# The RWKV recurrence of a two-layer decoder: a chunk's output turned by 64x64 identity products next to other 64x64 products, and y's last products moved beside the state's update

## The chip, the cores and the metric

The kernel runs on one NeuronCore of one Trainium2 chip. The metric is the device time of one execution in microseconds (us). Before the change it was 3168.34 us, the median of 3 runs that lay between 3163.14 and 3170.98. TensorE (PE) has a granted clock with two levels, 1.2 and 2.4 GHz, which the profile gives as 0.50 and 1.00.

## The reference, cut to what matters

Two layers on 2048 tokens of 1024 channels: sliding-window attention, then RWKV-7 time mixing, each followed by a gated embedding; a norm at the end. All is in float32. The change lies in the second layer, in the recurrence over tokens and the norm of its output per head:

```python
def step(S, inp):
    r_t, d_t, k_t, v_t, kk_t, a_t = inp
    sa = jnp.einsum('bhvk,bhk->bhv', S, -kk_t)
    S = S * d_t[:, :, None, :] + sa[..., None] * (kk_t * a_t)[:, :, None, :] + v_t[..., None] * k_t[:, :, None, :]
    y = jnp.einsum('bhvk,bhk->bhv', S, r_t)
    return S, y
...
y = ((y - mean) * lax.rsqrt(var + GN_EPS)).reshape(B, T, C) * gn_g + gn_b
y = (y + bonus.reshape(B, T, C)).astype(h.dtype)
return (y * jax.nn.silu(z)) @ w_out
```

## The kernel before, in words

The program has four phases: the projections of the attention layer, the attention, the projections of the RWKV layer, and `rwkv`, which is the phase of the change and runs from about 2000 us to the end.

In `rwkv` the 2048 tokens are 32 chunks of 64 tokens. The 16 heads are 8 pairs; the even head of a pair lives on partitions 0 to 63 and the odd one on 64 to 127 (`half`). What a chunk needs apart from the state is made ahead: `front` (masked products `aps`, transposes `tp`) for each chunk, and `tri` (inverses of triangular matrices, mostly small VectorE operations on `P` and `tmp`, and products `wq`) for four chunks at a time. The state then goes from chunk to chunk in `chain`, in five sets of 16 small products:

- `r1p` (L1307), what the chunk's tokens see of the state; ScalarE copies it to `r1`;
- the first part of `y` (L1313), from the state, 64x64 products, the even head's in one quarter of TensorE's array and the odd head's in the opposite one. I call it y's first products;
- `up` (L1317), the inverse times `r1`, also 64x64; VectorE and ScalarE copy it into `uv`;
- `sp` (L1324), the state's update, products of 128 rows and 64 columns; VectorE makes the next state from it (L1326, L1329) and GpSimd a copy (L1330);
- the last part of `y` (L1333), again 128 rows and 64 columns, added to the first in the one PSUM tile that `y` has. I call it y's last products.

Then `output` norms y: ScalarE squares (L1346), VectorE sums (L1348, L1349), GpSimd raises (L1350), VectorE scales y into `yc` (L1352). y's first products of the next chunk write the same PSUM tile, so they come after L1352 of this one. `yc` has tokens on partitions and has to be turned into [channel, token]: eight `transpose` instructions for the even heads (L1357) and eight products with an identity for the odd heads (L1358), taken in turn, into a PSUM tile `ytp`. `ytp` is one of three buffers of a pool that `aps`, `tp` and `wq` use too. VectorE multiplies it by a factor per channel (L1359), GpSimd adds and multiplies (L1361, L1362), and it goes to memory as `gated`.

Beside all that runs the generator `dense`: products of 128x128 weights with 512 tokens (`ps`, L567 to L569, three for each step because a float32 is split into two parts), which make z, the embeddings' projections, the output projection and the gate. One step of `dense` is a tick. `chain` calls `ticks(n)` between its sets of products, with n from `STEPS = (2, 2, 4, 3, 7)`, and at each tick every live generator (`front`, `tri`, `output`, `dense`) goes on to its next `yield`. So the written order of instructions comes from these counts; a scheduler in the framework then moves instructions within each engine by its own estimate of when their operands are ready. The order that results is the order of each engine's queue. VectorE, ScalarE and GpSimd run theirs in that order.

In `output` the ten yields ahead of the turning stand for ten ticks (four for the last chunk).

Of the kernel before, what the change touches and what calls it, by code (L numbers as in the profile page):

```python
# [16 lines left out]
T = 2048          # tokens  # L17
C = 1024          # channels
KT = C // 128     # 128-channel tiles
G = 512           # tokens of a group  # L20
# [27 lines left out]
def chan(ap, n):  # L48
    """A vector over channels as [128, n], channel = n_index * 128 + partition."""
    return ap.rearrange("(n p) -> p n", p=128)  # L50


class Dense:
    """A stream of matrix products with G tokens each, as a generator of steps (one k tile of one column of
    128): jobs (kind, n), whose operands of the tokens are fetched and split while the job before runs, and
    whose weights come in units of 8 steps."""

    def __init__(self, tr, es, name, jobs, side, raw=4, tmp=4, own=10, ps=2, lead=4):
        self.tr, self.nc, self.name, self.jobs = tr, tr.nc, name, jobs
        self.kinds = {}  # L60
        self.hp = tr.pool(es, name + "dh", 16, side=side)
        self.lp = tr.pool(es, name + "dl", 1, side=side)
        self.bufs = {"raw": raw, "t": tmp, "h": own, "m": ps}
        self.lead, self.cols_done, self.direct = lead, {}, {}
        # a job whose operands' last columns come from a tile on chip, [128, k, columns], once it is known
        self.late, self.rest = None, None
# [58 lines left out]
    def run(self):  # L125
# [5 lines left out]
        owner = []     # of each pair of operand tiles the last step that reads it  # L131
        for j, (kind, n) in enumerate(self.jobs):
            kt = self.kinds[kind].get("kt", KT)
            b = begin[kind, n] = 8 * len(units)
            units += [(kind, n, c) for c in range(self.kinds[kind].get("units", kt))]
            for k in range(kt):
                free = owner[len(owner) - KT] if len(owner) >= KT else -99
                if "after" in self.kinds[kind]:
                    # column k of that job, which has 8 units
                    fill = max(free + 1, begin[self.kinds[kind]["after"], n] + 8 * k + 8)  # L140
                else:
                    fill = max(free, b + k - 9) + 3
                    pre = 3 if "pre" in self.kinds[kind] else 0
                    if pre:
                        at(fill - pre, "pre", j, k)
                    at(fill - pre - self.lead, "fetch", j, k)
                assert fill <= b + k
                at(fill, "fill", j, k)
                if (kind, n) == self.late:
                    at(max(fill, b), "late", j, k)  # L150
                owner.append(8 * len(units) - kt + k)
# [6 lines left out]
        job = -1  # L158
# [48 lines left out]
    def add_ple(self, kind, i):  # L207
        """p @ w_proj / 2 of layer i."""
# [29 lines left out]
    def add_out(self, kind, w, src, res, ready, scale=None):  # L238
        """src @ w + res, which stay on chip for the job that follows; src is in memory or, as a function of the
        group and the k tile, on chip."""  # L240
# [10 lines left out]
    def add_rest(self, kind, src, m):  # L251
        """The last group's operands of a kind of jobs are in memory but for the last m columns."""
# [5 lines left out]
    def add_z(self, kind, w, src, dst):  # L258
        """Twice silu(lerp(src, src before, mu[3]) @ w)."""
# [12 lines left out]
        def pre(n, k, t):  # L272
            xs = self.tmp("xs")
            # GpSimd has other work while the phase starts
# [15 lines left out]
    def gated(self, th, ps, hl, ple, last=False):  # L290
        """h + sigmoid(ps) * 2 ple, where h = hi + lo."""
        nc = self.nc
        if last:
            # what does not need ps comes first
# [12 lines left out]
    def add_gate0(self, kind):  # L307
        """h2 = h1 + gated embedding of layer 0; hn1 = its norm."""
# [39 lines left out]
    def add_lora(self, kind):  # L348
        """Parts (float32r and the rest) of tanh(xw @ w1) and xa @ a1, from the products of hn1 and of hn1 a
        token earlier with weights that hold the lerps' factors."""  # L350
# [30 lines left out]
    def add_gate1(self, kind):  # L381
        """The result: the norm of h3 + gated embedding of layer 1."""
# [47 lines left out]
class Trunk:  # L430
# [40 lines left out]
    def consts(self):  # L471
        """Vectors of channels of the RWKV layer."""
# [21 lines left out]
    def lora_weights(self, pool, tag):  # L494
        """[w1 | a1] for hn1 a token earlier and for hn1, with the factors of the lerps."""
# [13 lines left out]
    def split(self, hi, lo, src, lo_engine="dve", scale=None):  # L509
        """hi (rounded to float32r) + lo = src exactly, or a power of two times it."""  # L510
# [9 lines left out]
    def rsqrt_rows(self, ss, s1, s2, op0, op1, pool, tag):  # L520
        """(ss op0 s1 op1 s2) ** -0.5 for a [128, G] PSUM tile whose rows are equal within each
        32 partitions: its 32 x 32 blocks are transposed so that only G / 32 columns are raised."""
# [12 lines left out]
    def operands(self, H, L, groups, pool):  # L535
        """Tiles (float32r and the rest) of the k tiles of groups of tokens."""
# [4 lines left out]
    # A phase is a generator: its first steps, which open the pools on the side of memory that the phase  # L541
    # before has left and start its first loads, run beside the end of that phase.
# [4 lines left out]
    # Work that goes on beside the matmuls is written as generators; each step of a matrix product  # L547
    # (one k tile) is a tick, in which every live one goes on to its next yield.
    def start(self, gen):
        """Runs gen to its first yield, and keeps it live."""  # L550
# [20 lines left out]
    def load_w(self, w, c0, lo_pool=None, lo_engine="dve"):  # L571
        """128 columns of a [C, n] weight as (hi, lo), [128, KT, 128] each."""
# [7 lines left out]
    def attn_proj(self):  # L580
# [8 lines left out]
        with ExitStack() as left, ExitStack() as right, ExitStack() as norms:  # L589
# [22 lines left out]
            def stats(n, wait=0):  # L612
                """1 / rms of a group's tokens, in a row that all partitions have."""
# [30 lines left out]
            def normed(n):  # L644
                """The group's operands: x transposed, normed and split."""
# [93 lines left out]
            for n in range(NG):  # L739
# [11 lines left out]
                # the first group's k tiles have just come about: all three products take each  # L751
# [27 lines left out]
    # ---- attention over blocks of 128 queries; beside it the embeddings' projections, the output  # L779
    # projection, the gated embedding of layer 0 and the norm of layer 1 ----  # L780
# [131 lines left out]
    def rwkv_proj(self):  # L912
# [6 lines left out]
        with ExitStack() as left, ExitStack() as right:  # L919
# [49 lines left out]
            def head_sums(sh, so):  # L969
                """Sums over each head's 64 channels, on all of its partitions (PSUM)."""  # L970
# [5 lines left out]
            def low_rank(j, nm, ct, n):  # L976
                """tanh(half of w0 + tanh(xw @ w1) @ w2) or of its like of a, in steps; n = 0 comes with the weights."""
# [35 lines left out]
            def evac_k(ps, ct, n):  # L1013
# [40 lines left out]
                # the products that the chunks' inverses need  # L1054
# [7 lines left out]
                # the diagonal 32 x 32 blocks of both halves of a chunk go into the same columns  # L1062
# [55 lines left out]
            for i, (c, evac) in enumerate(parts):  # L1118
                for pr in range(0, KT, 2):
                    if i or pr:  # L1120
                        ws = [self.load_w(w_in, c * C + ct * 128) for ct in (pr, pr + 1)]
                    for n in range(NG):
# [9 lines left out]
                        # the next part's operands: its first tiles are done with the last of this one, or,  # L1132
                        # where this one keeps the other engines busy, mostly with its own first
# [7 lines left out]
    # Of a pair of heads the even one lives on partitions 0-63 and the odd one on 64-127, so the  # L1141
    # operands stacked on 128 partitions are in the opposite order for the odd head.
    def rwkv(self):
# [9 lines left out]
        with ExitStack() as es:  # L1153
# [5 lines left out]
            # z is twice what it stands for  # L1159
# [23 lines left out]
            AM, X1, XA, BN, TT, UV, AG, BZ = {}, {}, {}, {}, {}, {}, {}, {}  # L1183

            def load_front(c):
# [5 lines left out]
                if c % 2 == 0:  # L1191
                    # [channel, pair, a or r, chunk, token] of two chunks
# [6 lines left out]
            def front(c):  # L1199
                """What chunk c needs apart from the state: masked products between its tokens, and the  # L1200
                transposes of x1."""
# [11 lines left out]
                # the products of the inverse are known: their place takes the operand of the state  # L1213
# [17 lines left out]
            def tri(g):  # L1231
                """Transposed inverses of I - A for the chunks of group g: first those of the 32 x 32
                diagonal blocks, one per partition (head, half of the chunk, pair, chunk)."""
# [65 lines left out]
            STEPS = (2, 2, 4, 3, 7)  # L1299

            def chain(c):
# [10 lines left out]
                for p, eo in pairs:  # L1312
                    mm(y[half[eo], p], lhsT=xa[half[eo], p, 1], rhs=uv[half[eo], eo, p], start=p == 0, stop=False)  # L1313
                self.ticks(STEPS[1])
# [16 lines left out]
                self.ticks(STEPS[3])  # L1331
# [3 lines left out]
                self.ticks(STEPS[4])  # L1335

            def load_bz(c):
                BZ[c] = tuple(r2.tile([128, NP, LC], F32, name=nm) for nm in ("bvt", "szt"))
                for t, src in zip(BZ[c], (bv, sz)):
                    nc.sync.dma_start(out=t, in_=src[:, c * LC:c * LC + LC].rearrange("(p q) t -> q p t", q=128))  # L1340

            def output(c, y):
# [10 lines left out]
                for _ in range(10 if c + 1 < NCH else 4):  # L1353
                    yield
                tp = p_f.tile([128, NP, LC], F32, name="ytp", tag="f")
                for p in range(NP):
                    nc.tensor.transpose(tp[half[0], p], yc[half[0], p], self.ident[half[0], half[0]])  # L1357
                    nc.tensor.matmul(tp[half[1], p], lhsT=yc[half[1], p], rhs=self.ident[half[1], half[1]], start=True, stop=True)  # L1358
# [63 lines left out]
```

## Time and profile before

| | |
|---|---|
| median of 3 runs | 3168.34 us |
| span of the profiled execution | 3165.9 us |
| PE matmul busy | 2989.6 us (94%) |
| VectorE busy | 2099.7 us (66%) |
| ScalarE busy | 1439.7 us (45%) |
| GpSimd busy | 1023.0 us (32%) |
| DMA, mean rate | 168 GB/s |
| stretch of the recurrence | about 2000 to 3040 us |
| dense products alone after it | 3040 to 3165.9 us |

The profiled execution's span, from its first to its last instruction, is 2.4 us under the median of the runs. Busy PE time is not PE at its peak, because products overlap; how fast a set of products goes is read from the difference between starts in the timeline. A float32 product is two PE instructions (two passes), so 16 products of a set stand as 32 instructions; a transpose is one. Line numbers are those of the kernel before.

### The profile page before, as it was taken

The numbers are of one execution on the slowest core, as the hardware profiler recorded it, in microseconds if no ns is written. First come the engines' busy times: TensorE is split into PE (matmuls) and PEld (weight loads), VectorE is DVE, ScalarE is ACT, GpSimd is POOL, SyncE is SP. The second block draws the span as 40 slices with busy tenths as digits, with TensorE's granted clock in tenths as the row PEclk, the third lists the DMA queues.
The fourth block names the chain that finished last, engine by engine and source line by source line (L and its number), as shares of the span: only waits on it lengthen the run. The fifth ranks groups of instructions, "written<-read, shape, count | busy, mean of one in ns | idle before, by whom it ended". The sixth has DMA issues, their size and how long they took to land. (4 is left out here: it accounts for less than half of the span.)

```text
span 3165.9 us, 55911 instructions
## 1 busy us (share of the span) xinstructions
PE 2989.6 (94%) x21160; PEld 2346.0 (74%) x21160; DVE 2099.7 (66%) x3665; ACT 1439.7 (45%) x2976; POOL 1023.0 (32%) x886
## 2 busy tenths in 40 slices
PE   7999997999999998898998899999999999999997
PEld 5888886777777776686776687777777777777776
DVE  6533434766888766747778867688777587684455
ACT  5311114864675544526677633333333443443433
POOL 2233500002211333305556501124634444453421
PEclk9999998999999989999998999998999999989999
DMA  7665838875674555636556778855566566566463
GB/s 217 191 134 119 170 124 222 234 203 168 160 200 114 163 174 163 190 117 196 178 198 203 219 201 211 232 142 140 145 161 144 131 158 169 132 157 161 108 190 93
DMA packets 704030, 532.84 MB, mean 168 GB/s; under 512 B 255504, under 2 KB 558736, under 8 KB 703760
## 3 DMA queue, kind: packets, MB, share of 16 engines
q1 hardware_dynamic: 696080, 518.76, 59.0%
q0 software_dynamic: 7680, 10.50, 3.0%
q8 instruction: 167, 2.74, 0.4%
q14 instruction: 103, 0.84, 0.1%
HBM read 350.09 MB, written 168.56 MB: 164 GB/s over the span
## 5 line engine op out<-in xcount | busy, mean ns | idle before, releaser
L567 PE MATMUL ps<-dhi,dwh 128*128 128x512 f32 x1472 | 614.9, 420 | 19.5 <-ACT dwh L516 14.6
L569 PE MATMUL ps<-dhi,dwl 128*128 128x512 f32 x1472 | 598.8, 407 | 12.1 <-DVE dwl L518 11.5
L568 PE MATMUL ps<-dlo,dwh 128*128 128x512 f32 x1472 | 599.0, 408 | 4.1 <-DVE dlo L518 2.5
L567 PE MATMUL ps<-xH,wh 128*128 128x512 f32 x1408 | 555.1, 401 | 20.4 <-DVE kb L1049 7.6
L568 PE MATMUL ps<-xL,wh 128*128 128x512 f32 x1408 | 559.8, 398 | 1.8 <-DVE xL L518 1.4
L569 PE MATMUL ps<-xH,wl 128*128 128x512 f32 x1408 | 560.4, 398 | 0.8 <-DVE wl L518 0.8
L567 PEld LDWEIGHTS ps<-dhi,dwh 128*128 128x128 f32 x1472 | 285.5, 194 | 90.9 <-ACT dwh L516 16.0
L569 PEld LDWEIGHTS ps<-dhi,dwl 128*128 128x128 f32 x1472 | 285.2, 194 | 80.5 <-DVE dwl L518 14.9
L568 PEld LDWEIGHTS ps<-dlo,dwh 128*128 128x128 f32 x1472 | 286.3, 194 | 63.5 <-POOL dlo L518 4.6
L567 PEld LDWEIGHTS ps<-xH,wh 128*128 128x128 f32 x1408 | 268.4, 192 | 83.1 <-DVE kb L1049 11.5
L568 PEld LDWEIGHTS ps<-xL,wh 128*128 128x128 f32 x1408 | 270.1, 192 | 61.6 <-DVE xL L518 2.4
L569 PEld LDWEIGHTS ps<-xH,wl 128*128 128x128 f32 x1408 | 269.4, 191 | 59.0 <-DVE wl L518 1.7
L518 DVE TENSOR_TENSOR dwl<-wraw,dwh 128x1024 fp32r<-128x1024 f32 x152 | 194.4, 1279 | 120.6 <-ACT dwh L516 113.8
L516 ACT ACTIVATE dwh<-wraw 128x1024 fp32r<-128x1024 f32 x152 | 160.5, 1056 | 202.4 <-PE ps L568 138.5
L677 POOL DMA_DIRECT2D t<-t x160 | 126.0, 1255 | 201.2 <-issue 78.8
L851 ACT ACTIVATE S<-S,nm 128x256 f32<-128x256 f32 (+1 forms) x256 | 125.6, 494 | 68.8 <-DVE nm L848 62.9
L518 POOL TENSOR_TENSOR xL<-xs,xH 128x512 fp32r<-128x512 f32 x72 | 111.2, 1554 | 69.3 <-ACT xH L516 68.9
L516 ACT ACTIVATE wh<-wr 128x1024 fp32r<-128x1024 f32 x44 | 46.6, 1060 | 185.8 <-DMA wr<-in_attn_w_in 141.4
L842 DVE CUSTOM_DVE_ANT_0 S<-sc,mask,sink 128x256 f32<-128x256 f32 (+1 forms) x256 | 109.0, 468 | 20.8 <-PE sc L838 20.7
L1247 DVE TENSOR_TENSOR tmp<-P 128x30 f32<-128x30 f32 (+14 forms) x240 | 111.7, 465 | 9.3 <-POOL P L1238 3.4
L953 DVE SCALAR_TENSOR_TENSOR xs<-hp,mu,xs 128x512 f32<-128x512 f32 x96 | 94.1, 991 | 31.1 <-ACT xs L952 30.6
L1249 DVE TENSOR_TENSOR P<-P,tmp 128x30 f32<-128x30 f32 (+14 forms) x240 | 108.8, 454 | 6.4
(260 smaller groups left out, 5517.8 us busy)
## 6 DMA issues: line engine op xcount, KB each, us to landing
wraw<-in_ple_w_gate SPq DMA_DIRECT2D x64, 512.0 KB, 4.0
hp<-hn SPq DMA_DIRECT2D x72, 256.5 KB, 4.0
sz<-th SPq DMA_DIRECT2D x64, 256.0 KB, 4.5
ple<-pt SPq DMA_DIRECT2D x64, 256.0 KB, 6.0
wraw<-in_attn_w_out SPq DMA_DIRECT2D x32, 512.0 KB, 4.0
aux<-ple SPq DMA_DIRECT2D x64, 256.0 KB, 3.8
yd<-kx SPq DMA_DIRECT2D x32, 512.0 KB, 4.4
wraw<-in_rwkv_w_in SPq DMA_DIRECT2D x32, 512.0 KB, 5.3
```

Of the source, the lines that this page charges most:

```text
L516: nc.scalar.activation(hi, src, AF.Copy)
L518: e.tensor_tensor(out=lo, in0=src, in1=f32(hi), op=ALU.subtract)
L567: mm(ps, lhsT=wh, rhs=ah, start=first, stop=False)
L568: mm(ps, lhsT=wh, rhs=al, start=False, stop=False)
L569: mm(ps, lhsT=wl, rhs=ah, start=False, stop=last)
L677: nc.gpsimd.dma_start(out=t1[32 * d:32 * d + 32, :], in_=t2[32 * a:32 * a + 32, :], accum_op=ALU.add)
L842: nc.vector.tensor_tensor_reduce(out=S[:, i, c0:], in0=sc[:, eo, c0:], in1=mask[:, c0:], scale=1.0, scalar=sink[:, 4 * g + 2 * j + eo:4 * ...
L851: nc.scalar.activation(S[:, i, c0:], S[:, i, c0:], AF.Exp, bias=nm[:, i:i + 1], accum_out=den[:, i:i + 1])
L953: nc.vector.scalar_tensor_tensor(out=src, in0=t[:, :G], scalar=mus[:, c, k:k + 1], in1=src, op0=ALU.mult, op1=ALU.add)
L1247: nc.vector.tensor_tensor(out=t, in0=P[:, 0:r, r:r + 1].broadcast_to([128, r, n]), in1=P[:, r:r + 1, r + 1:].broadcast_to([128, r, n]), op ...
L1249: nc.vector.tensor_tensor(out=P[:, 0:r, r + 1:], in0=P[:, 0:r, r + 1:], in1=t, op=ALU.add)
```

## The change

- `output` no longer issues the turning itself, but for the last chunk. It puts `yc` into a table and yields until the turned tile is there.
- A new function `turn` turns a chunk with 16 identity products, for the even and odd heads alike; no `transpose` is left. `chain` of the next chunk calls it right after y's first products.
- `chain` issues y's last products right after the state's update, without the three ticks between them; the three are added to the seven at the end.

```diff
-            STEPS = (2, 2, 4, 3, 7)
+            STEPS = (2, 2, 4, 10)
...
                 for p, eo in pairs:
                     mm(y[half[eo], p], lhsT=xa[half[eo], p, 1], rhs=uv[half[eo], eo, p], start=p == 0, stop=False)
+                if c:
+                    turn(c - 1, YC.pop(c - 1))
                 self.ticks(STEPS[1])
...
                     nc.gpsimd.tensor_tensor(out=S, in0=t, in1=d, op=ALU.mult)
-                self.ticks(STEPS[3])
                 for p, eo in pairs:
                     mm(y[half[eo], p], lhsT=am[:, p, eo, LC:], rhs=uv[:, eo, p], start=False, stop=p == NP - 1)
                 self.start(output(c, y))
-                self.ticks(STEPS[4])
+                self.ticks(STEPS[3])
...
+            def turn(c, yc):
+                tp = YT[c] = p_f.tile([128, NP, LC], F32, name="ytp", tag="f")
+                for p in range(NP):
+                    for h in half:
+                        nc.tensor.matmul(tp[h, p], lhsT=yc[h, p], rhs=self.ident[h, h], start=True, stop=True)
...
-                for _ in range(10 if c + 1 < NCH else 4):
-                    yield
-                tp = p_f.tile([128, NP, LC], F32, name="ytp", tag="f")
-                for p in range(NP):
-                    nc.tensor.transpose(tp[half[0], p], yc[half[0], p], self.ident[half[0], half[0]])
-                    nc.tensor.matmul(tp[half[1], p], lhsT=yc[half[1], p], rhs=self.ident[half[1], half[1]], start=True, stop=True)
+                if c + 1 < NCH:
+                    YC[c] = yc
+                    while c not in YT:
+                        yield
+                else:
+                    for _ in range(4):
+                        yield
+                    turn(c, yc)
+                tp = YT.pop(c)
```

The rest of the diff is comments.

Two places of PE's queue show what moves. In its rows x16 counts 16 equal products in a row (each is two instructions in the trace).

The first is in the chain of chunk 12, which turns the output of chunk 11; `tp` is the front's transposes, `y<-uv,xa` are y's first products. Before:

```order
L1226 MATMUL tp<-ident,x_22758 128x128 x4
L1313 MATMUL y<-uv,xa 64x64 x16
L567 MATMUL ps<-dhi,dwh 128x512
L568 MATMUL ps<-dlo,dwh 128x512
L569 MATMUL ps<-dhi,dwl 128x512
L1357 MATMUL ytp<-ident,yc 64x64
L1358 MATMUL ytp<-ident,yc 64x64
```

and seven more pairs of L1357 and L1358, four transposes `tp` and one dense step follow ahead of `up`. Now:

```order
L1226 MATMUL tp<-ident,x_22758 128x128 x4
L1313 MATMUL y<-uv,xa 64x64 x16
L1348 MATMUL ytp<-ident,yc 64x64 x16
L567 MATMUL ps<-dhi,dwh 128x512
L568 MATMUL ps<-dlo,dwh 128x512
L569 MATMUL ps<-dhi,dwl 128x512
```

The dense step that stood between y's first products and the turning now comes after both, so the 32 products of 64x64 stand in one piece. Of the 31 turnings that `chain` calls, 28 stand right behind y's first products like this; three early ones stand a few rows later.

The second is around the state's update of chunk 18, where `wq` are `tri`'s 32x32 products. Before:

```order
L1268 MATMUL wq<-at,ag 32x32 x9
L1278 MATMUL wq<-tt,wt 32x32 x16
L1324 MATMUL sp<-uv,bn 64x64 x16
L1268 MATMUL wq<-at,ag 32x32 x7
L1333 MATMUL y<-uv,am 64x64 x16
L568 MATMUL ps<-dlo,dwh 128x512
```

and now:

```order
L1268 MATMUL wq<-at,ag 32x32 x14
L1278 MATMUL wq<-tt,wt 32x32 x16
L1268 MATMUL wq<-at,ag 32x32 x2
L1326 MATMUL sp<-uv,bn 64x64 x16
L1334 MATMUL y<-uv,am 64x64 x16
L567 MATMUL ps<-dhi,dwh 128x512
```

The update and y's last products stand in one piece now. In about one chunk of four they stood apart before; in the others the scheduler had put 15 of the 16 y products behind the update already. Counted along PE's queue from the recurrence's first `aps` to the end, the shape of the products (128x128 with any number of columns, 128x64, 64x64, 64x128, 32x32) changes 611 times before and 547 times now.

## Rows read from the trace of the kernel before

**Rows 1.** The page: its first line, and PE's line of the busy times.

```profile
span 3165.9 us, 55911 instructions
PE 2989.6 (94%) x21160; PEld 2346.0 (74%) x21160; DVE 2099.7 (66%) x3665; ACT 1439.7 (45%) x2976; POOL 1023.0 (32%) x886
```

**Rows 2.** Windows: stretch, us; busy us (instructions) of five engines; granted clock; DMA share; GB/s.

```profile
2000.00:3040.00 1040.00, 1005.08 (x11133) 775.24 (x11134) 735.94 (x1131) 399.91 (x810) 437.92 (x360) 0.93 0.60 150
3040.00:3165.90 125.90, 106.16 (x461) 83.94 (x459) 68.21 (x89) 42.15 (x122) 22.59 (x16) 0.93 0.50 147
2111.80:2327.30 215.50, 207.81 (x2439) 162.19 (x2438) 180.59 (x281) 78.04 (x135) 110.49 (x92) 0.89 0.57 142
2327.30:3018.60 691.30, 675.74 (x7711) 519.35 (x7710) 460.20 (x695) 271.38 (x582) 294.45 (x240) 0.94 0.59 146
```

**Rows 3.** PE's waits, 2000 to 3040 us: total us, times, longest us.

```profile
PE ps L569 <- DVE dwl L518: 6.8, 5, 2.4
...
PE y L1313 <- DVE yc L1352: 2.2, 1, 2.2
PE aps L1208 <- ACT am L1211: 1.8, 1, 1.8
```

**Rows 4.** PE's timeline in chunk 12: start us, us to the group's last end, what.

```profile
2436.24 1.15 PE L1313 MATMUL y<-uv,xa 64*64 64x64 f32 x32
2437.32 0.50 PE L567 MATMUL ps<-dhi,dwh 128*128 128x512 f32 x1
2437.66 0.40 PE L568 MATMUL ps<-dlo,dwh 128*128 128x512 f32 x1
2437.89 0.39 PE L569 MATMUL ps<-dhi,dwl 128*128 128x512 f32 x1
2438.21 0.24 PE L1357 MATMUL ytp<-ident,yc 64*64 64x64 f32 x1
2438.39 0.33 PE L1358 MATMUL ytp<-ident,yc 64*64 64x64 f32 x2
2438.64 0.24 PE L1357 MATMUL ytp<-ident,yc 64*64 64x64 f32 x1
...
2441.63 0.66 PE L1226 MATMUL tp<-ident,x 128*128 128x128 f32 x4
...
2443.41 1.97 PE L1317 MATMUL up<-r,tt 64*64 64x64 f32 x32
2445.32 0.65 PE L567 MATMUL ps<-dhi,dwh 128*128 128x512 f32 x1
```

**Rows 5.** The instructions on `ytp`: duration ns min/median/max, first and last start.

```profile
L1358 PE MATMUL ytp<-ident,yc x512: 218/267/365, 2113.1 to 3039.0; 64*64 64x64 f32 x171
L1357 PE MATMUL ytp<-ident,yc x256: 241/242/313, 2113.0 to 3038.8; 64*64 64x64 f32 x128
```

**Rows 6.** Windows of about 3.4 us: chunk 12's turning and the two after it.

```profile
2438.20:2441.60 3.40, 3.40 (x25) 2.34 (x24) 3.19 (x7) 0.00 (x0) 1.49 (x2) 1.00 0.22 64
2442.30:2445.60 3.30, 3.30 (x36) 2.43 (x36) 3.03 (x11) 0.59 (x1) 0.78 (x1) 0.50 0.49 114
2445.70:2449.10 3.40, 3.40 (x16) 2.71 (x16) 3.40 (x3) 0.75 (x1) 1.75 (x2) 1.00 0.62 131
```

**Rows 7.** Windows right behind the first and the last turning that a fall follows.

```profile
2170.00:2173.40 3.40, 3.40 (x38) 2.81 (x35) 1.76 (x4) 0.59 (x1) 2.84 (x4) 0.50 0.02 5
3039.60:3043.00 3.40, 3.40 (x10) 2.63 (x9) 3.19 (x5) 1.06 (x2) 0.84 (x1) 0.50 0.90 283
```

**Rows 8.** Windows of whole chunks, `up` to `up`: chunks 12, 16, 24 and, light, 10.

```profile
2415.90:2443.40 27.50, 27.50 (x279) 21.16 (x278) 26.48 (x52) 8.30 (x13) 9.42 (x8) 0.93 0.56 116
2535.00:2565.10 30.10, 30.10 (x291) 23.55 (x290) 28.59 (x51) 11.92 (x36) 10.62 (x10) 0.90 0.47 111
2784.80:2814.60 29.80, 29.80 (x292) 23.45 (x292) 28.68 (x51) 11.74 (x34) 10.73 (x10) 0.91 0.51 115
2356.00:2383.40 27.40, 27.40 (x336) 20.85 (x335) 7.86 (x13) 10.11 (x17) 10.76 (x10) 0.95 0.57 131
```

More of the change, by code (lines that the diff above doesn't have):

```diff
@@ L1182, in rwkv @@
             half = (slice(0, 64), slice(64, 128))
-            AM, X1, XA, BN, TT, UV, AG, BZ = {}, {}, {}, {}, {}, {}, {}, {}
+            AM, X1, XA, BN, TT, UV, AG, BZ, YC, YT = {}, {}, {}, {}, {}, {}, {}, {}, {}, {}
             def load_front(c):
```

## The prediction, made before the changed kernel ran

> **What bounds the kernel now.** I read the page first: PE is busy for 94% of the span, every other engine for much less [rows 1]. Then the windows by stage [rows 2]. The recurrence, 2000 to 3040 us, has PE busy for 1005 of 1040 us; VectorE, the next, for 736. The 126 us behind it have no small products and are not touched. PE's waits for others inside the recurrence are small: the longest group is 6.8 us in total, and the wait of y's first products for the scaled chunk, which the change leans on, is 2.2 us, once [rows 3]. So in this stage time is what PE's instructions take, one behind the other, and what its clock grants: 0.93 of full speed on average [rows 2].
>
> The timeline of one chunk shows where PE's time goes [rows 4]. Read the differences of starts. Y's first products, 32 instructions, take 2437.32 - 2436.24 = 1.08 us. The turning, 24 instructions with as many outputs, takes 2441.63 - 2438.21 = 3.42 us: eight times 0.43 us, of which the transpose has 2438.39 - 2438.21 = 0.18 and the odd head's product (two passes) 2438.64 - 2438.39 = 0.25. In y's first products the two heads of a pair overlap; in the turning nothing overlaps. Its instructions are not long in themselves (242 and 267 ns at the median [rows 5]); they are far apart.
>
> Last, the clock. In the turning it is at 2.4 GHz, right behind it at 1.2 GHz for one stretch, then back [rows 6]. I asked this for all 32 turnings: behind 24 of them the clock falls, the first and last of these in [rows 7], for 3.4 to 7.9 us each, 107 us together. The whole recurrence has about 2 x (1 - 0.93) x 1040 = 146 us at half clock [rows 2], so the turnings precede most of it. What it costs: `up`, a set like y's first products, takes 2445.32 - 2443.41 = 1.91 us at the low level against 1.08, a factor of 1.77 [rows 4].
>
> **The change part by part.**
>
> *The turning as 16 identity products.* They have the shape of y's first products, with both halves in turn, 32 instructions: 1.08 us by that row instead of 3.42. 32 chunks x 2.34 = 75 us less, all on PE's path. Bounds: 1.08 if the halves overlap; 16 x 0.25 = 4.0 us if they don't. I take 1.08, since the row has the same shape and the same order of halves.
>
> *Fewer changes of shape.* A dense step behind another starts 0.23 us later; the first instruction of the turning starts 2438.21 - 2437.89 = 0.32 us behind the last dense one, and the second dense one behind y's products starts 0.34 us behind the first [rows 4]. So a change costs about 0.10 us each way. There are 64 fewer (611 to 547): -6 us. Most come from the turning; y's last products were already next to the update in most chunks, so that part is worth 1 to 2 us. The Trainium skill, TensorEngine Tiling (Array Packing), Key Properties, says that changing the tiling mode drains the engine; were a drain a whole instruction's 0.24 us [rows 5], the term would be -15. The rows show less than half of that, and the sum goes by them.
>
> *The clock.* If what fills the turning's place keeps PE as densely fed as its other sets, the 107 us go back to full speed: 107 x (1 - 1/1.77) = -47 us. Bounds: 0 if small products of any kind let it fall, -53 if all of it were halved.
>
> *New waits.* `turn` needs `yc`; so does y's first set right ahead of it, through the PSUM tile that it overwrites. So the turning waits for nothing that PE had not waited for already (2.2 us today). What stands behind it, `up` and the dense steps, comes nearer to `r1`, which ScalarE copied some 7 us earlier in PE's queue. A buffer for `ytp` is one of three that ScalarE empties; the like wait of `aps` is 1.8 us, once [rows 3], and a turning holds it for less time than before. I cost both at nothing. The square, sum and scaling of y come up to three ticks earlier and have 12 ticks ahead of y's next set instead of 9; the last multiply, GpSimd's two operations and the store come about where they came before, and the output projection that reads them begins many chunks later. Nothing there.
>
> *What is late next: VectorE.* The sum so far is -75 - 6 - 47 = -128 us, 4.0 us for each chunk. Every fourth chunk runs `tri`'s 60 operations on VectorE and is nearly full: 26.5 of 27.5, 28.6 of 30.1 and 28.7 of 29.8 us, 95 to 96%, against 7.9 of 27.4 in a light one [rows 8]. Such a chunk cannot give 4 us; at 97 to 98% busy it gives 1. Four late ones of this kind hand back 4 x 3 = 12 us. In the z stage VectorE has 180.6 us of 215.5 [rows 2]; its eight chunks would shrink by 32 to 183.5, and at the 95% of the full chunks it stays at 190: 7 back. Waits for splits and copies, some 10 us today in the largest groups [rows 3], will grow as PE comes earlier; I add 7. Give-back 26, with ends 0 (the queue shifts its work into the light chunks) and 52 (twice as much).
>
> Sum: -128 + 26 = -102 us. The profiled execution's span is 3165.9 us, 2.4 under the median; from the median, **3066 us**, -3.2%. A measurement of this kernel can tell about 0.3%, 10 us, from no change.
>
> **The rivals.**
>
> 1. *VectorE takes no toll* (0.20): light and full chunks even out over its queue. For: its mean is 736 of 1040 us [rows 2], 81% of a stage shorter by 128. Against: its queue runs in order, and PE's next state comes out of it. 3168 - 128 = 3040.
>
> 2. *The clock does not come back* (0.12): two 64x64 sets in a row feed few columns too. For: the turning had small products as well. Against: `up` ran in the low stretch and the window behind it is at 1.00 [rows 6]. Then -81 and, since chunks shrink by 2.5 us alone, a give-back of some 10: 3097.
>
> 3. *The halves do not overlap* (0.04), the one on the other side. Place: the 16 identity products. Each would keep 0.25 us, 4.0 for a chunk instead of 3.42, since a product has two passes where a transpose has one: 32 x 0.6 = +19, -6 for the changes of shape, and the clock falls as before: 3181. It decides from 0.21 us for a product (3.42 / 16). Against it is y's first set, 0.07 us for a product [rows 4]; for it, that `ytp` products have never stood side by side. The Trainium skill, TensorE: Matmul & The Clock Gate, Terms, has a transpose mode that is four times faster for float32, which would speak against this change; four times the transpose's 0.18 us for each of 16 products without overlap would be 11.5 us a chunk and 3420 in all. The trace disagrees: a product keeps PE 0.25 us, 1.4 times the transpose.
>
> 4. *It does not do what it says* (0.02): new waits swallow it all. The queue's order shows the products where the change puts them, and a wait would need 4 us in each chunk, against 2.2 once. No change.
>
> **How the numbers follow.** The forecast has the remaining 0.62: 3066 within its give-back bounds, 3045 to 3092. The range reaches to rival 1 and rival 2 with some room for the clock's and the shape changes' bounds: 3030 to 3105, which leaves out rivals 3 and 4 and the tails. Faster by over 0.3%: the forecast and rivals 1 and 2, 0.94; within 0.3%: 0.02; slower: 0.04.
>
> **What would show it.** In the changed profile the turning should be one group of 32 instructions in about 1.1 us right behind y's first set; no transposes of `yc`; the recurrence's granted clock near 0.98, with falls only behind PE's waits; the recurrence some 100 us shorter, and the 126 us behind it as they were. PE's waits should grow, with VectorE as the releaser and in the chunks with `tri`. I am wrong if the identity products stand at 0.25 us each, if the clock still falls behind them, or if VectorE's share stays below 95% in full chunks while PE waits for something else.

## The result, and the profile after

The changed kernel takes 3124.64 us (median of 4 runs, 3120.12 to 3131.41), the one before 3166.36 beside it (4 runs): a ratio of 0.9868 with a 95% interval of 0.9846 to 0.9889, so 42 us or 1.3% less. I had forecast 3066, in a range of 3030 to 3105. The direction was right; more than half of the gain did not come.

The page of the changed kernel, against [rows 1] (the line numbers in a view of a run are those of that run's kernel):

```profile
span 3123.0 us, 56427 instructions
PE 2885.0 (92%) x21416; PEld 2284.2 (73%) x21416; DVE 2112.2 (68%) x3665; ACT 1438.3 (46%) x2976; POOL 1023.5 (33%) x886
```

PE lost 105 us of busy time, of the 128 that I had taken off it, but the span fell by 43 only. So most of the missing time is not on PE's instructions: PE waits instead.

The timeline of PE in the chain of chunk 12, the place of [rows 4]:

```profile
2428.62 1.15 PE L1313 MATMUL y<-uv,xa 64*64 64x64 f32 x32
2429.60 1.10 PE L1348 MATMUL ytp<-ident,yc 64*64 64x64 f32 x32
2430.63 0.50 PE L567 MATMUL ps<-dhi,dwh 128*128 128x512 f32 x1
...
2432.66 1.15 PE L1319 MATMUL up<-r,tt 64*64 64x64 f32 x32
2433.74 0.51 PE L567 MATMUL ps<-dhi,dwh 128*128 128x512 f32 x1
```

The turning takes 2430.63 - 2429.60 = 1.03 us instead of 3.42: its halves overlap like those of y's first products. `up` takes 1.08 instead of 1.91, because the clock does not fall. The windows of the turning and right behind it, against [rows 6] (columns as there: busy us of PE, PE's weight loads, VectorE, ScalarE, GpSimd; clock; DMA):

```profile
2428.60:2432.00 3.40, 3.40 (x73) 3.13 (x73) 3.30 (x5) 1.56 (x3) 3.29 (x4) 1.00 0.50 148
2432.00:2435.40 3.40, 3.40 (x43) 2.65 (x42) 3.12 (x9) 0.59 (x1) 0.63 (x1) 1.00 0.53 121
```

Behind none of the 32 turnings does the clock fall now; before it was 24. So the turning itself and the end of the falls behind it came as forecast.

PE's waits, 2000 to 3000 us, against [rows 3] (in total, times, longest):

```profile
PE y L1334 <- DVE uv L1320: 15.6, 7, 4.9
PE ps L399 <- DVE th L305: 14.8, 8, 5.6
PE ps L569 <- DVE dwl L518: 10.2, 7, 3.3
PE aps L1208 <- DVE tt L1282: 10.1, 4, 3.3
...
PE aps L1208 <- DVE yc L1370: 5.5, 2, 2.9
```

Here `uv` is the copy of `up`, `th` belongs to an embedding's gate, `dwl` to the split of the dense weights; `tt` and `yc` are written by VectorE out of PSUM buffers that `aps` needs next. All rows of this view add up to 95 us, where those of the recurrence before added up to 35. VectorE (DVE) is the releaser in 84 of the 95 us. The recurrence up to its last turning, against [rows 2]:

```profile
2000.00:2987.50 987.50, 893.24 (x11373) 708.95 (x11372) 741.09 (x1126) 394.15 (x797) 432.65 (x355) 0.95 0.64 156
```

Where the waits fall is seen by cycles of four chunks. First the kernel before, then the changed one; three cycles with `tri` each, and in the fourth row the last four chunks, for which no `tri` runs:

```profile
2535.00:2660.60 125.60, 123.39 (x1399) 94.82 (x1398) 90.64 (x130) 51.97 (x131) 57.28 (x46) 0.92 0.70 174
2660.60:2784.80 124.20, 118.55 (x1382) 90.95 (x1382) 93.51 (x157) 46.86 (x97) 49.94 (x43) 0.94 0.53 127
2784.80:2910.30 125.50, 122.46 (x1391) 93.98 (x1390) 85.34 (x123) 48.96 (x113) 58.95 (x47) 0.91 0.67 170
2910.30:3018.60 108.30, 108.30 (x1091) 83.60 (x1090) 52.48 (x70) 42.83 (x99) 38.22 (x31) 0.95 0.42 106
```

```profile
2516.10:2637.80 121.70, 109.51 (x1431) 86.21 (x1430) 93.22 (x137) 52.15 (x132) 54.53 (x41) 0.96 0.77 181
2637.80:2758.60 120.80, 107.71 (x1413) 85.42 (x1412) 96.22 (x151) 46.55 (x97) 52.83 (x46) 0.93 0.56 129
2758.60:2879.30 120.70, 107.57 (x1421) 84.20 (x1420) 89.86 (x133) 49.21 (x114) 57.39 (x45) 0.96 0.73 176
2879.30:2972.70 93.40, 93.40 (x1127) 74.84 (x1128) 53.85 (x70) 42.83 (x100) 40.44 (x33) 1.00 0.55 133
```

The last four chunks lost 14.9 us, 3.7 for each, nearly the 4.0 of the sum without give-back. The cycles with `tri` lost 3.9, 3.4 and 4.8 us, about one for each chunk. PE's busy time fell by 11 to 15 us in those as well, and became waiting. VectorE is busy for only 74 to 80% of such a cycle, so its mean does not show what holds PE up. The first of these cycles by chunks, from one `up` to the next, before and then after:

```profile
2535.00:2565.10 30.10, 30.10 (x291) 23.55 (x290) 28.59 (x51) 11.92 (x36) 10.62 (x10) 0.90 0.47 111
2565.10:2595.30 30.20, 28.89 (x289) 21.92 (x288) 21.42 (x31) 12.19 (x36) 11.64 (x11) 0.95 0.69 175
2595.30:2627.30 32.00, 31.09 (x352) 23.52 (x351) 21.34 (x24) 17.00 (x41) 25.76 (x20) 0.93 0.60 149
2627.30:2660.60 33.30, 33.30 (x476) 25.84 (x472) 19.29 (x26) 10.86 (x20) 9.26 (x8) 0.91 1.00 254
```

```profile
2516.10:2546.40 30.30, 27.19 (x301) 21.59 (x300) 29.65 (x53) 11.49 (x32) 9.15 (x8) 0.94 0.65 145
2546.40:2578.10 31.70, 25.10 (x297) 19.45 (x296) 26.25 (x39) 12.74 (x39) 13.09 (x11) 1.00 0.57 146
2578.10:2610.50 32.40, 29.92 (x361) 23.41 (x360) 22.85 (x25) 17.15 (x42) 26.39 (x19) 0.89 0.81 191
2610.50:2637.80 27.30, 27.30 (x483) 21.77 (x480) 14.47 (x22) 10.77 (x21) 5.91 (x5) 1.00 1.07 249
```

Now VectorE is busy for 98 and 83% of the first two, which hold most of this cycle's elimination and its block transposes. PE waits 3.1 and 6.6 us in them and 2.5 us in the third. None of the three got shorter; the whole gain of the cycle is in the fourth.

The timeline of VectorE in chunk 16 of the changed kernel shows what stands ahead of PE's operands:

```profile
2554.77 2.01 DVE L1255 STREAM_TRANSPOSE at<-P 128x1024 f32<-128x1024 f32 x1
2556.63 2.23 DVE L1256 STREAM_TRANSPOSE tt<-P 128x1024 f32<-128x1024 f32 x1
2558.75 2.31 DVE L1258 STREAM_TRANSPOSE tt<-P 128x1024 f32<-128x1024 f32 x1
2560.93 1.23 DVE L518 TENSOR_TENSOR dwl<-wraw,dwh 128x1024 fp32r<-128x1024 f32 x1
2562.03 0.73 DVE L303 SCALAR_TENSOR_TENSOR th<-th,aux 128x512 f32<-128x512 f32 x1
2562.63 0.73 DVE L1328 TENSOR_TENSOR st<-sp,S 128x512 f32<-128x512 f32 x1
```

and PE beside it, with its waits in brackets:

```profile
2554.71 1.15 PE L1326 MATMUL sp<-uv,bn 128*64 128x64 f32 x32
...
2562.22 0.50 PE L569 MATMUL ps<-dhi,dwl 128*128 128x512 f32 x1 [1.72 <-DVE dwl L518]
...
2566.87 0.63 PE L399 MATMUL ps<-ident,th 128*128 128x128 f32 x4 [2.60 <-DVE th L305]
```

At the end of `tri` three transposes of 2 us stand in one row in VectorE's queue, and behind them the split of the dense weights (`dwl`) and the state (`st`). The state's products started at 2554.71; `st`, which needs them, came 8 us later, and `th` later still.

Two things follow from the waits. The clock now falls behind them instead of behind the turnings: each of the 16 low stretches of the recurrence begins behind waits of PE. One of them:

```profile
2644.50:2647.90 3.40, 0.96 (x3) 0.48 (x3) 3.30 (x8) 0.00 (x0) 0.74 (x1) 1.00 0.08 24
2647.90:2658.10 10.20, 5.96 (x68) 5.12 (x69) 9.79 (x21) 2.24 (x3) 1.79 (x2) 0.50 1.01 174
```

In 3.4 us in which PE had 0.96 us to do the clock was at 2.4 GHz, then at 1.2 for 10.2 us. And the end of the program, which I had taken to be untouched, grew. From the last turning's end to the program's end, first before, then after:

```profile
3039.30:3165.90 126.60, 106.86 (x462) 84.50 (x462) 68.91 (x90) 42.15 (x122) 23.29 (x16) 0.93 0.50 148
```

```profile
2987.50:3123.00 135.50, 110.52 (x476) 86.78 (x476) 75.00 (x93) 46.62 (x137) 28.00 (x20) 0.92 0.49 146
```

9 us more: two more dense steps and eight other PE instructions are left there, and PE waits 4.9 us for one split (`dwl`, L514), with a low stretch of 6.8 us around it.

### The profile page after: what moved, and what is told of

It reads as the page before. It is cut to its first block, busy times and chain, and to the rows that moved or that the text cites. A ratio compares the mean times of both kernels' runs of the same rounds, so it can differ in the third digit from the quotient of the medians.

```text
span 3123.0 us, 56427 instructions
## 1 busy us (share of the span) xinstructions
PE 2885.0 (92%) x21416; PEld 2284.2 (73%) x21416; DVE 2112.2 (68%) x3665; ACT 1438.3 (46%) x2976; POOL 1023.5 (33%) x886
```

## Experiments

Theory A: the terms on PE came as forecast, and VectorE's queue in the chunks with `tri` took most of them back. Theory B: the new place of the turning costs time on PE's own queue. Theory C: y's last products, issued early, make PE wait. Each kernel ran beside the kernel before on the same chip, whose medians there were between 3164.93 and 3165.50.

**mixed_turn: the new place, but transposes again for the even heads.**

```diff
-                    for h in half:
-                        nc.tensor.matmul(tp[h, p], lhsT=yc[h, p], rhs=self.ident[h, h], start=True, stop=True)
+                    nc.tensor.transpose(tp[half[0], p], yc[half[0], p], self.ident[half[0], half[0]])
+                    nc.tensor.matmul(tp[half[1], p], lhsT=yc[half[1], p], rhs=self.ident[half[1], half[1]], start=True, stop=True)
```

> The changed kernel, but the even heads are turned by transposes again, in turn with the odd heads' products, at the new place. Theory A (the identity products give what was forecast, 2.3 us a chunk and the clock behind it, and VectorE's full chunks take most of it back): the turning is 3.4 us again, the clock falls behind it again, and the time goes back to about 3160, within 10 us of the kernel before. Theory B (the new place of the turning costs part of the gain, since it stands ahead of the next products of the chain): clearly slower than before, 3180 or more. If the new place alone gives the 42 us, it stays near 3125.

Measured: 3164.97 us, ratio 0.9999 (0.9980 to 1.0019). Its timeline has the slow turning back, and the low clock behind it:

```profile
2423.83 0.24 PE L1347 MATMUL ytp<-ident,yc 64*64 64x64 f32 x1
2424.00 0.33 PE L1348 MATMUL ytp<-ident,yc 64*64 64x64 f32 x2
...
2427.25 0.51 PE L567 MATMUL ps<-dhi,dwh 128*128 128x512 f32 x1
2427.59 0.59 PE L568 MATMUL ps<-dlo,dwh 128*128 128x512 f32 x1
2427.97 0.63 PE L569 MATMUL ps<-dhi,dwl 128*128 128x512 f32 x1
```

2427.25 - 2423.83 = 3.42 us, and behind 21 of the 32 turnings the clock falls. So at the new place the whole gain is that of the identity products in place of the transposes, and with transposes the new place, together with the moved part of y, is worth nothing either way; theory B, which asked for 3180 or more, is out. Identity products at the old place were not run, so whether the place counts once the turning is short is not shown.

**y_back: the changed kernel, y's last products three ticks after the update again.**

```diff
-            STEPS = (2, 2, 4, 10)
+            STEPS = (2, 2, 4, 3, 7)
...
+                self.ticks(STEPS[3])
                 for p, eo in pairs:
                     mm(y[half[eo], p], lhsT=am[:, p, eo, LC:], rhs=uv[:, eo, p], start=False, stop=p == NP - 1)
                 self.start(output(c, y))
-                self.ticks(STEPS[3])
+                self.ticks(STEPS[4])
```

> The changed kernel, but y's last products come three ticks after the state's update again. Theory A: they were next to the update in most chunks anyway, so within 6 us of the changed kernel, 3119 to 3131. Theory C (y's last products, issued early, make PE wait for the copies of up on VectorE, 15.6 us in the changed kernel's trace, and so take back part of the gain): 10 to 20 us faster than the changed kernel, 3105 to 3115.

Measured: 3119.42 us, ratio 0.9851 (0.9834 to 0.9868), whose interval overlaps that of the changed kernel. PE's wait for `uv` is still there with 12.6 us, so theory C is out. The recurrence is no faster (its last turning ends at 2991.8 us instead of 2987.5), but the end is shorter:

```profile
2991.80:3119.90 128.10, 106.70 (x464) 84.69 (x462) 71.97 (x91) 45.31 (x135) 25.81 (x18) 0.94 0.50 148
```

128.1 us against 135.5. The second half of the change gains nothing in the recurrence, and in these two profiles the longer end goes with it; the medians can't separate 5 us.

**before_half and after_half: every second row of the elimination left out of `tri`, in both kernels.**

```diff
+                    if r % 2:
                         nc.vector.tensor_tensor(out=t, in0=P[:, 0:r, r:r + 1].broadcast_to([128, r, n]),
...
                         nc.vector.tensor_tensor(out=P[:, 0:r, r + 1:], in0=P[:, 0:r, r + 1:], in1=t, op=ALU.add)
```

> The kernel before without every second row of tri's elimination on VectorE (30 of its 60 operations left out for each four chunks; the ticks stay). Theory A: before the change PE was the bound nearly everywhere, so little is gained, 10 to 30 us: 3136 to 3156.

> The changed kernel with the same half of tri's rows left out. Theory A (VectorE's full chunks took back the rest): the difference to the like kernel before grows from 42 to 90 or more, so 3030 to 3060. Theory B or C (the rest was lost on PE's own queue, whatever VectorE does): the difference stays near 42 to 55, so about 3090 to 3105.

Measured: before_half 3164.27 us, ratio 0.9996 (0.9980 to 1.0012); after_half 3085.43, ratio 0.9743 (0.9727 to 0.9760). Half of the elimination is worth nothing to the kernel before and 39 us to the changed one. The change itself is worth 79 us with it away, against 42. Both expectations missed: before_half gained nothing where I had expected 10 to 30 us, and after_half lies between the two ranges. The difference of 79 is nearer to the 90 of theory A than to the 42 to 55 of the rivals, so VectorE's work in `tri` takes back a large part of the gain.

**after_notri and before_notri: all 60 operations of the elimination left out.**

```diff
-                for r in range(30, 0, -1):
...
+                for _ in range(15):
+                    yield
```

> The changed kernel without any of the 60 elimination operations of tri (its ticks, its transposes of 32x32 blocks and its products stay). Theory A (VectorE's load in tri's chunks took the gain back): the half cut was worth 39 us more to the changed kernel and nothing to the one before, so the full cut should reach the forecast without give-back, about 3040 (3030 to 3055). If the three block transposes of 2 us each, which stand in one row on VectorE, matter as much as the elimination, it stops at 3065 to 3080.

> The kernel before without tri's 60 elimination operations, the control to the same cut of the changed kernel (3030, 135 us under before). Theory A (PE bounds the kernel before; VectorE's chunks only begin to count once the turning is short): 0 to 15 us faster than before, 3150 to 3166, so that the change is worth 120 us or more where VectorE has room. If VectorE's load in tri's chunks was a bound already before the change, it is 40 us or more faster, under 3125, and the change itself is worth less than 95.

Measured: after_notri 3030.32 us, ratio 0.9560 (0.9523 to 0.9597); before_notri 3128.34, ratio 0.9881 (0.9848 to 0.9913). The change is worth 98 us by these medians. The recurrence of after_notri, up to its last turning, and that of before_notri:

```profile
2000.00:2892.20 892.20, 857.62 (x11337) 679.01 (x11336) 547.32 (x644) 393.20 (x794) 438.41 (x355) 0.98 0.71 172
```

```profile
2000.00:3009.70 1009.70, 991.29 (x11096) 760.53 (x11096) 547.16 (x648) 397.74 (x809) 438.04 (x359) 0.93 0.61 152
```

With VectorE's load at 547 us on both sides the recurrence shrinks by 117.5 us in these two profiles and the clock goes from 0.93 to 0.98, the 0.98 of the forecast without give-back; the end grows by 8 us here too. The profiled execution of before_notri lies 9.5 us above its median and that of after_notri 2.3 under it, so by medians the recurrence gives nearer to 106 than 117.5, against 128 in the forecast. My expectation for before_notri, at most 15 us, was a miss: it gained 37, near the 40 of the rival that VectorE was a bound already before the change, and 98 is near that rival's 95 too. So theory A holds in part only: some of VectorE's load already cost time before. In before_notri PE waits 18 us in the recurrence (1009.70 - 991.29) instead of 35; in before_half it still waits 36. Why the second half of the rows mattered there and the first didn't, I did not follow up. Leaving operations out also changes the order of the queues. The two small edits of the kernel before further down cost 16 and 19 us, so a part of that size of these differences could be the order.

**after_spread and before_spread: `tri` over more ticks.**

```diff
-                    if r % 2:
+                    if r % 3:
                         yield
...
                 nc.vector.transpose(at.rearrange("q p c s -> q s (p c)"), P)
+                yield
```

> The changed kernel with all of tri's work, spread over more ticks: three rows of the elimination in two ticks instead of four, and a tick between the first two block transposes. Theory A1 (it is the evenness of VectorE's load that counts): 10 to 30 us faster than the changed kernel, 3095 to 3115. Theory A2 (its sum over a whole cycle of four chunks counts, or the scheduler places the rows by its own estimate whatever the ticks): 3118 to 3130.

> The kernel before with the same spread. Under both theories PE bounds it, so it stays within 10 us of the kernel before: 3156 to 3176.

Measured: after_spread 3121.26 us, ratio 0.9849 (0.9809 to 0.9888), no difference to the changed kernel; before_spread 3180.93, ratio 1.0059 (1.0030 to 1.0088), where I had expected no change. So this spread of the ticks is no cure. This doesn't separate the two readings of A2: the scheduler may place the rows as before, or the sum over a cycle may count.

**after_uvact and before_uvact: both copies of `up` on ScalarE.**

```diff
-                nc.vector.tensor_copy(uv[half[0], 0], up[half[0]])
+                nc.scalar.copy(uv[half[0], 0], up[half[0]])
```

> The changed kernel with both halves of the copy of up on ScalarE, so that the state's update does not stand behind tri's rows in VectorE's queue there. Theory A: PE's wait for this copy (15.6 us in the changed kernel's trace) goes, the waits behind st and the splits stay: 5 to 15 us faster than the changed kernel, 3110 to 3120. If ScalarE's own queue is as late, no difference: 3120 to 3130.

> The kernel before with both halves of the copy of up on ScalarE. Theory A: the edit gave the changed kernel 12 us because VectorE was late there; before the change it is not, so no difference, 3160 to 3170. If the copy is simply better on ScalarE, 10 us or more faster here as well.

Measured: after_uvact 3112.24 us, ratio 0.9817 (0.9779 to 0.9855); before_uvact 3184.09, ratio 1.0051 (1.0027 to 1.0075). A copy of 0.68 us for each chunk taken from VectorE's queue gives about 12 us in the changed kernel by the medians (the intervals just overlap), and costs 0.5% in the kernel before, where I had expected no difference. The largest wait of the changed kernel is gone from the list of its waits, and the next is nearly as large:

```profile
PE ps L399 <- DVE th L305: 15.5, 9, 3.7
PE r1p L1307 <- DVE uv L1331: 10.0, 7, 4.6
PE ps L569 <- DVE dwl L518: 9.2, 5, 3.4
```

**uvact_yback and after_acts: two versions built on it.** The first has y_back's edit as well, the second puts `tri`'s copies `wt` and `tt` on ScalarE too:

```diff
-                        cpy = nc.vector.tensor_copy if e else nc.scalar.copy
+                        cpy = nc.scalar.copy
```

> The changed kernel with the copies of up on ScalarE and y's last products three ticks after the update again. Each alone gave 3112 and 3119; if both gains are real and add, 3104 to 3110; if the second is within the spread between programs, 3110 to 3118.

> The changed kernel with the copies of up and tri's copies wt and tt all on ScalarE, 0.7 us a chunk and 3.4 us for four chunks less on VectorE. Theory A (each microsecond taken from VectorE in tri's chunks counts): a few us under the 3112 of the copy of up alone, 3103 to 3110. If only the place of the state's copies in the queue counts: 3110 to 3116; if ScalarE's queue now holds up tri: over 3116.

Measured: uvact_yback 3108.65 us, ratio 0.9821 (0.9797 to 0.9844), no clear step. after_acts 3104.72, ratio 0.9802 (0.9778 to 0.9826), 20 us under the changed kernel with intervals apart: the fastest version that computes everything, 1.9% under the kernel before. It fits theory A, which has it that time taken from VectorE counts wherever it stands in these chunks, but its step of 8 us from after_uvact is not shown, since those two intervals overlap.

## Why the prediction was wrong, by its own steps

- *The turning as 16 identity products*, -75 us: right. 1.03 us against 1.08 forecast, and mixed_turn shows that the gain hangs on it. Rival 3 (halves that don't overlap) fell with it. The Trainium skill, TensorE: Matmul & The Clock Gate, Terms, gives a transpose mode that is four times faster for float32. No run here shows that factor: in turn a product keeps PE 0.25 us and a transpose 0.18 [rows 4], and 16 products alone took a third of the time of 8 transposes and 8 products.
- *Fewer changes of shape*, -6 us: not tested by itself. The moved half of y's part was worth nothing (y_back), as its 1 to 2 us would have it.
- *The clock*, -47 us: half right. The 24 falls behind the turnings are gone, and where PE has no one to wait for the clock is at 1.00 (the last four chunks). But I assumed that nothing else would let it fall. By the granted clock of the recurrence the low time went from 146 us [rows 2] to some 99 (2 x 0.05 x 987.5; the clock is rounded to 0.01, which is 10 us either way), so new falls behind PE's waits took back about half of what the turnings had cost. The 107 us were a little low: two of the 24 falls, from 2169.2 and from 2268.2 us, last 13.7 us each and not 7.9 at most, which makes about 119 us in all and a term of -52.
- *What is late next: VectorE*, +26 us: this is the step that failed. The mechanism was named, but the term was mis-sized: of its 26 us only 7 were for longer waits, where PE's waits alone grew by 60 us (95 against 35). In the profiles the account closes. PE's busy time in the recurrence fell by 112 us (1005.08 in [rows 2], 893.24 in the row of the result) and not by 128, the new falls of the clock among the 16 that are missing; the waits took 60 and the end 9. That makes 85, which is 128 less the 43 us of the span. Two readings were at fault. I took `tri`'s 60 operations to fill every fourth chunk; in the trace of before they stand in two or three chunks of every four (21, 30 and 9 of them in the stretches from 2500.3, 2535.0 and 2565.1 us), with the three block transposes behind them. And I priced the longer waits at 7 us, though by the timeline of chunk 16 the split, the state and `th` that PE needs stand behind those operations in VectorE's queue. So a cycle with `tri` gave about 1 us a chunk instead of 4. The runs without the elimination bring 56 us of it back (98 - 42 by medians). The other 30 are not assigned by a run; 8 of them are the longer end.
- *The 126 us behind the recurrence are not touched*: wrong by 9 us in the profile. Work that the recurrence no longer covers is left for the end, and a split was late there.
- *New waits: I cost both at nothing*: wrong. `y`'s last products, and the state's update behind them, wait for `uv` behind VectorE's queue, which I had not listed. The buffer of `ytp` is emptied by VectorE, not by ScalarE as I wrote, and `aps` now waits 5.5 us for that; in mixed_turn this wait does not occur.
- The range ended at 3105 because I doubled the give-back at most; the measured one was more than three times the 26. (Its ends of 0 and 52 give 3040 to 3092, where I wrote 3045 to 3092.) Of the rivals, 1 (no toll, 128 us) is not reached even without the elimination (98 us), and 2 is out: the clock did come back behind the turnings.

## What to carry to other kernels

When an instruction group on the bounding engine gets shorter, ask in each stage what the in-order queues of the other engines hold ahead of the results that it needs; a mean busy share of 75% gave no such room here. Look for where the suspected load stands, chunk by chunk, and compare a repeating unit of the program with and without it (here the last four chunks, for which `tri` is over: they gave 3.7 us each, the others about 1). And transposes in turn with small products can cost, as a set, three times what plain products with an identity cost.

## What the runs showed of the hardware

- Eight transposes and eight identity products in turn take 3.42 us, sixteen identity products 1.03, though each of those is two instructions: in turn the two halves of the array don't overlap, as products alone they do. The low clock stood behind 24 of 32 turnings of the first kind and behind none of the second.
- In the kernel before, small moves in order (before_spread, before_uvact) cost 0.5 to 0.6%: the first adds no work to any engine, the second moves a copy of 0.68 us a chunk from VectorE to ScalarE. before_uvact has a granted clock of 0.949 over its span against 0.954; in its recurrence PE is no busier (1003 us) but waits 51 us instead of 35. Why the order makes it wait longer there, and what slows before_spread, stays open.
